# Modulation products on four quarters of TensorE's array, and products of ones at eleven places of a three-layer kernel

## The chip, the cores and the metric

One core of one Trainium2 chip runs the whole kernel in one launch. The metric is the device time of one execution in microseconds (us), as the median of several runs; lower is better.

## The reference

512 tokens of width 1024 (and 256 context tokens) go through a first block and then two layers of a second block, all in float32. Cut to what matters here:

```python
def first_block(x, c, ctx, c_ctx, w_mod, b_mod, ...):
    mod_x = (silu(c) @ w_mod + b_mod).reshape(-1, 6, d)       # 1024 x 6144
    mod_c = (silu(c_ctx) @ w_mod[:, :2*d] + b_mod[:2*d])
    hx = modulate(rms_norm(x, g_mix), mod_x[:, 0], mod_x[:, 1])   # h * (1 + scale) + shift
    hc = modulate(rms_norm(ctx, g_mix), mod_c[:, 0], mod_c[:, 1])
    x = x + mod_x[:, 2] * hybrid_mixer(hx, hc, ...)           # projections, three attentions, merge
    hx = modulate(rms_norm(x, g_ffn), mod_x[:, 3], mod_x[:, 4])
    x = x + mod_x[:, 5] * expert_choice_ffn(hx, ...)          # 16 experts take their top 64 tokens
    return rms_norm(x, g_final)

def second_block(x, c, ctx, c_ctx, mod_w, mod_b, ...):        # two layers
    for l in range(2):
        mod, mod_c = silu(c) @ mod_w[l] + mod_b[l], silu(c_ctx) @ mod_w[l] + mod_b[l]   # 1024 x 3072
        x, xc = trunk_layer(x, xc, mod, mod_c, ...)           # rmsnorm, modulate, projections, three
    return x                                                  # branches (mla, pool, gla), merge, residual
```

The modulation vectors (`mod`) are products of two vectors (c and c_ctx) with large weight matrices; everything that follows a norm needs its part of them.

## The kernel before, in words

**Layout.** The activations lie transposed: eight chunks of 128 features, each 128 x 512 tokens (`hx`, `x`), or 128 x 256 for the context (`hc`). A weight tile of 128 x 1024 float32 is loaded by the queue of SP, cut by ScalarE into a high part `wh` and by VectorE into the rest `wl`, and each product is three matmuls (`mm3`, L404 to L406): high by high, high by rest, rest by high. A projection is eight such triples into one PSUM tile. Matmuls on plain float32 (`modblock`, the norm sums, transposes, the router) are not split.

**Modulation.** `modblock` computes one block of `mod`: 16 weight tiles of 512 KB for a width of 2048 columns (8 tiles for 1024), 96 tiles in all. `sc` holds the two vectors padded to 32 columns, so that one matmul needs 32 of the array's 128 columns; a tile is multiplied in two matmuls of 512 columns (L471) whose results lie in PSUM rows 32j to 32j+31, with j alternately 0, 1 and 2, 3. Then ScalarE copies the sums to SBUF (`mrow`, L477), TensorE turns them (L480), VectorE adds the bias. The first block (16 tiles) runs at the start, ahead of everything that needs a modulated input; its tiles come through a ring of 7 buffers. Of the other 80 tiles, 56 are paced between the first block's projections (a ring of 3 buffers), and 24 between its merge and its output projection (a ring of 6).

**Order.** The code is a set of generators. `drain` runs one to its end; `weave`, `pace`, `alt` and `Fill` interleave two or more by estimated costs. A scheduler then orders the instructions of each engine by priority; each engine runs its own in that order and waits at an instruction whose inputs are not there. `s.late(...)` keeps an instruction where the program has it in relation to the others of its engine.

**Chains that TensorE waits for.** They are at the norms and at the router:
- `rstd_c` sums squares over features (L497), ScalarE and VectorE take the root and its reciprocal `rs`, TensorE transposes and spreads it (`bcast`, L533), ScalarE copies it to `rb`, and VectorE and ScalarE make `hx` of it (`normmod`, L567 to L570).
- `block1_mixer` (L1090 on) ends with `rstd_c`; `ffn_start` (L1261) then modulates, runs `router` (L1209, eight matmuls that lie on the four quarters in turn), turns the tokens back (L1278) and stores them to memory, and runs `topk` (eight rounds on VectorE, then four small matmuls L1252 and L1253). `experts` gathers the chosen tokens by a DMA with an index (`gather`, tile `xg`), turns them (`turn`, L1321) and runs the experts (L1306).
- `ffn_end` ends with `turned` and `rstd_col`; `xstart` (one for each layer of the second block, l = 0 and l = 1) spreads the root and makes `hx`. For l = 1 the sums (L516) come chunk by chunk behind the residual `o` (L2001, L2002), go through one row `sr` (L524), `rs` and L533.
- `xrest` ends with `merge(2, YG, ...)`, the merge of the gla branch: eight output chunks, each four triples of matmuls `ps<-yg,wh`. Three of the four `yg` inputs exist early; the fourth comes out of the last head of `gla` (L1910, L1911), its norm (L497, L533) and a split (L395).

Of the kernel before, what the change touches and what calls it, by code (L numbers as in the profile page):

```python
# [15 lines left out]
D = 1024  # L16
# [301 lines left out]
class Kern:  # L318
# [39 lines left out]
    def P1(s, tag, w=512):  # L358
        return s.pp.tile([128, w], F32, name=s.uid("ps"), tag=tag, bufs=PS[tag])

    def mm(s):
        return s.P1("mm")

# [96 lines left out]
    def modblock(s, sc, src, width, dst, bias, col0, big=None, ps=None):  # L460

        nc = s.nc
        ps = s.mm() if ps is None else ps
        nj = width // 512
        for k in range(8):
            for j in range(nj):
                if j % 2 == 0:
                    w = s.wp.tile([128, 1024], F32, name=s.uid("wr"), tag="wraw", bufs=NRAW) if big is None else \
                        big.tile([128, 1024], F32, name=s.uid("wm"), tag="wbig", bufs=s.nbig)
                    nc.sync.dma_start(w, src[k][:, j * 512:j * 512 + 1024])  # L470
                nc.tensor.matmul(ps[32 * j:32 * j + 32, :], sc[:, k, :], w[:, j % 2 * 512:j % 2 * 512 + 512],  # L471
                                 start=k == 0, stop=k == 7)
                if j % 2:
                    yield 0.9
        n = 32 * nj
        rows = s.T(nm="mrow", tag="t5")
        nc.scalar.copy(rows[:n], ps[:n])  # L477
        pt = s.at()
        for i in range(4):
            nc.tensor.transpose(pt[:, i * 128:i * 128 + n], rows[:n, i * 128:i * 128 + 128],  # L480
                                s.const("ident")[:n, :n])
        pv = pt.rearrange("p (i j v) -> p j i v", i=4, j=4)
        for v in range(2):
            o = dst[:, v, col0:col0 + 4 * nj].rearrange("p (j i) -> p j i", j=nj)
            b = bias[:, col0:col0 + 4 * nj].rearrange("p (j i) -> p j i", j=nj)
            nc.vector.tensor_tensor(o, pv[:, 0:nj, :, v], b, ALU.add)
        yield 0.5


# [600 lines left out]
    def block1_mixer(s, xd, M, ctx2):  # L1090
# [6 lines left out]
        rx = s.rstd_sb(s.sqsum(x, 512), D, 512)  # L1097
        with s.pool("bigA") as big:
            s.nbig = 7
            drain(s.modblock(sc, s.d["wmod0"], 2048, mod, bm, 0, big))  # L1100
        A1 = s.cp.tile([128, 2, 8], F32, name="A1")
        for v in range(2):
            nc.vector.scalar_tensor_tensor(A1[:, v, :], mod[:, v, 8:16], 1.0, s.const("gmix"), ALU.add, ALU.mult)
# [90 lines left out]
        def put(c, ps):  # L1194
            nc.vector.scalar_tensor_tensor(x[c], ps, m2h[:, c:c + 1], x[c], ALU.mult, ALU.add)
            s.load(xd[c], x[c])
            acc[0] = s.sqadd(acc[0], x[c], 512)
        drain(alt(s.outproj(hl, s.d["wout"], 512, put), mods, 2))
        return x, s.rstd_c(acc[0], D, 512)


# [32 lines left out]
    def topk(s):  # L1234
# [3 lines left out]
        for r in range(CAP // 8):  # L1238
            q = slice(8 * r, 8 * r + 8)
            nc.vector.max(vals[0:16, q], wk[0:16])  # L1240
            nc.vector.max_index(idx[0:16, q], vals[0:16, q], wk[0:16])
            nc.vector.match_replace(wk[0:16], vals[0:16, q], wk[0:16], -1.0)
            yield 2.0
        idf = A("idf")
        nc.vector.tensor_copy(idf[0:16], idx[0:16])
        s.gate, s.idx128 = A("gate", 8), s.cp.tile([128, 8], U32, name="idx128")
# [13 lines left out]
    def ffn_start(s, x, r):  # L1260

        nc = s.nc
        rb = s.T(nm="rb", tag="t5")
        nc.scalar.copy(rb, s.bcast(r, "t5"))
        yield 3.0
        for k in range(8):
            h = x[k]
            nc.vector.tensor_tensor(h, h, rb, ALU.mult)
            nc.scalar.activation(h, h, AF.Identity, bias=s.mod[:, 0, 24 + k:25 + k], scale=s.A2[:, k:k + 1])
            yield 0.6  # L1270
        h2 = x
        yield from s.router(h2)
        s.h2d = s.dram([512, D])
        for t in range(4):
            for g in range(2):
                pt = s.at()
                for j in range(4):
                    nc.tensor.transpose(pt[:, j * 128:j * 128 + 128], h2[4 * g + j][:, t * 128:t * 128 + 128],  # L1278
                                        s.const("ident"))
                o = s.T(nm="ht", tag="t5")  # L1280
                nc.scalar.copy(o, pt)
                nc.scalar.dma_start(s.h2d[t * 128:t * 128 + 128, g * 512:g * 512 + 512], o)
            yield 1.0
        yield from s.topk()

    def experts(s):
# [37 lines left out]
            return xe  # L1324

        xg = gather(0)
        xe = turn(xg)
        for p in range(8):
            if p < 7:
# [67 lines left out]
    def ffn_end(s, xd):  # L1397
# [25 lines left out]
            yield 1.2  # L1423

        s1, s2 = s.turned(ps, 2, 512, "ft")
        r1 = s.rstd_col(s1, D, 4)
        r2 = s.rstd_col(s2, D, 4, r1)
        rr = s.S("rr")
# [624 lines left out]
    def xstart(s, l, M, C, x, acc, xd, fill, done=None):  # L2053

        nc = s.nc
        if l == 0:
            rr, r1 = acc
            rb = s.T(nm="rb")
            nc.scalar.copy(rb, s.bcast(rr))
            a = s.cp.tile([128, 8], F32, name="Ag")  # L2060
            nc.vector.tensor_tensor(a, M["A"][:, 0, :], s.const("gfin"), ALU.mult)
        else:
            rb, a = s.T(nm="rb"), M["A"][:, 0, :]
            nc.scalar.copy(rb, s.bcast(s.rstd_col(s.turned(acc, 1, 512)[0], D, 4)))
        fill.step(5.0)
        hx = s.normmod(x, 512, a, M["S"][:, 0, 0:8], lambda: s.TT(512, "hx", "hx"), rb)
        fill.step(5.0)
# [14 lines left out]
    def xrest(s, l, M, C, hx, st, qn, gd, gt, xd, out, fill):  # L2082
# [14 lines left out]
        s.where2 = (None, {})  # L2097
        fill.flush()
        hl = []
        drain(s.merge(2, YG, s.d[f"wbr{l}"], gd, md, 512, hl, "hx"))  # L2100
        return s.finish(l, M, 0, hl, 512, lambda c: xd[c], (lambda c: xd[c]) if out is None else lambda c: out[:, c, :],
                        out is None)
# [113 lines left out]
```

## Time and profile before

| | before |
|---|---|
| time, median of 3 runs | 2761.48 us (2756.41 to 2765.88) |
| profiled execution: time | 2770.7 us |
| profiled execution: span on the core | 2768.9 us |
| mean granted TensorE clock over the span | 0.975 |
| TensorE busy | 95% of the span |
| VectorE, ScalarE, GpSimd busy | 57%, 44%, 6% |

The span is the stretch from the first to the last instruction of the core. The granted clock is a share of 2.4 GHz; 0.5 is 1.2 GHz. A matmul in float32 leaves two records in the trace, as do the transposes; a row that says x4 can be two matmuls.

### The profile page before, as it was taken

How to read it: one execution, taken by the hardware profiler on the slowest of the kernel's cores; microseconds unless marked ns; L12 is line 12 of the kernel's file. 1: busy time of each engine (PE TensorE's matmuls, PEld its weight loads, DVE VectorE, ACT ScalarE, POOL GpSimd, SP SyncE). 2: the span in 40 equal slices, each digit the busy share in tenths (PEclk: the TensorE clock that was granted, in tenths of full speed). 3: DMA queues.
4: the chain of work that ended last, by engine and by line, in shares of the span. 5: the costliest groups of instructions: out<-in, count | busy, mean ns of one | idle time of the engine just before them, and what ended most of it. 6: DMA issues, size and time to landing. Idle time of an engine off the chain costs nothing. (4 is left out here: it accounts for less than half of the span.)

```text
span 2768.9 us, 41759 instructions
## 1 busy us (share of the span) xinstructions
PE 2618.2 (95%) x16372; PEld 1858.0 (67%) x16372; DVE 1570.1 (57%) x2957; ACT 1230.5 (44%) x2159; POOL 159.6 (6%) x260
## 2 busy tenths in 40 slices
PE   6999999999968999998998899999999999999997
PEld 2666677887633566555654577777777777777776
DVE  3565576676451324455332665657976456766974
ACT  2333354445231224365222454546655544555652
POOL 1000001110001000000000000000010000000001
PEclk8899999999979999999999899999999999999998
DMA  8545424543979999988999332213453332114353
GB/s 281 180 162 202 141 81 173 187 134 121 326 289 336 351 392 353 335 312 292 354 374 380 119 117 74 77 54 136 136 192 129 123 122 82 57 47 137 119 175 116
DMA packets 167974, 537.68 MB, mean 194 GB/s; under 512 B 21272, under 2 KB 22376, under 8 KB 167776
## 3 DMA queue, kind: packets, MB, share of 16 engines
q1 hardware_dynamic: 138528, 460.40, 46.7%
q0 software_dynamic: 17152, 52.57, 5.9%
q10 hardware_dynamic: 12096, 22.03, 2.1%
q8 instruction: 129, 2.11, 0.3%
q14 instruction: 69, 0.57, 0.1%
HBM read 484.06 MB, written 48.76 MB: 192 GB/s over the span
## 5 line engine op out<-in xcount | busy, mean ns | idle before, releaser
L391 DVE TENSOR_TENSOR wl<-wr,wh 128x1024 fp32r<-128x1024 f32 x320 | 390.6, 1223 | 353.8 <-ACT wh L395 330.3
L395 ACT CAST wh<-wr 128x1024 fp32r<-128x1024 f32 x320 | 334.2, 1047 | 428.2 <-PE ps L405 339.8
L404 PE MATMUL ps<-hx,wh 128*128 128x512 f32 x1168 | 473.2, 406 | 5.8 <-ACT hx L569 5.1
L405 PE MATMUL ps<-hx,wh 128*128 128x512 f32 x1168 | 468.4, 401 | 0.1
L406 PE MATMUL ps<-hx,wl 128*128 128x512 f32 x1168 | 466.3, 400 | 0.0
L404 PEld LDWEIGHTS ps<-hx,wh 128*128 128x128 f32 x1168 | 221.7, 190 | 66.0 <-issue 12.4
L405 PEld LDWEIGHTS ps<-hx,wh 128*128 128x128 f32 x1168 | 221.4, 190 | 51.6 <-issue 8.0
L406 PEld LDWEIGHTS ps<-hx,wl 128*128 128x128 f32 x1168 | 221.3, 189 | 50.1 <-issue 5.0
L1306 PE MATMUL ps<-we,xe 128*64 128x512 f32 x1024 | 236.7, 606 | 10.5 <-DMA we<-in_wexp 10.5
L673 ACT ACTIVATE P<-ps,st 128x768 f32<-128x768 f32 (+3 forms) x144 | 111.1, 771 | 143.4 <-DVE st L669 107.3
L1306 PEld LDWEIGHTS ps<-we,xe 128*64 128x64 f32 x1024 | 72.8, 139 | 134.9 <-issue 112.9
L404 PE MATMUL ps<-hc,wh 128*128 128x256 f32 x496 | 144.7, 293 | 0.2 <-ACT wh L395 0.2
L406 PE MATMUL ps<-hc,wl 128*128 128x256 f32 x496 | 141.3, 285 | 0.7 <-DVE wl L391 0.6
L405 PE MATMUL ps<-hc,wh 128*128 128x256 f32 x496 | 141.4, 286 | 0.0
L667 DVE TENSOR_REDUCE st<-ps 128x1 f32<-128x768 f32 (+3 forms) x144 | 114.2, 793 | 36.0 <-PE ps L406 33.1
L1306 PE MATMUL ps<-we,hT 128*64 128x512 f32 x512 | 119.6, 612 | 6.6 <-DMA we<-in_wexp 5.2
L695 PE MATMUL ps<-c_ident,P 128*128 128x128 f32 x688 | 109.8, 278 | 5.3 <-ACT PT L698 3.5
L404 PEld LDWEIGHTS ps<-hc,wh 128*128 128x128 f32 x496 | 95.0, 192 | 20.3 <-issue 16.6
L695 PEld LDWEIGHTS ps<-c_ident,P 128*128 128x128 f32 x688 | 79.9, 140 | 39.6 <-ACT PT L698 13.4
L471 PE MATMUL ps<-wm,sc_cc 128*32 128x512 f32 x384 | 90.8, 664 | 16.1 <-DMA wm<-in_wmod 14.7
L698 ACT COPY PT<-ps 128x512 f32<-128x512 f32 x123 | 70.1, 586 | 72.8 <-PE ps L695 72.0
L405 PEld LDWEIGHTS ps<-hc,wh 128*128 128x128 f32 x496 | 95.2, 192 | 5.6 <-issue 5.2
(517 smaller groups left out, 5032.1 us busy)
## 6 DMA issues: line engine op xcount, KB each, us to landing
we<-in_wexp SPq DMA_DIRECT2D x384, 512.0 KB
wr<-in_win SPq DMA_DIRECT2D x240, 512.0 KB
wm<-in_wmod SPq DMA_DIRECT2D x48, 512.0 KB
wr<-in_wbr SPq DMA_DIRECT2D x48, 512.0 KB
dram<-th ACTq DMA_DIRECT2D x72, 256.0 KB
mth<-dram SPq DMA_DIRECT2D x72, 256.0 KB
wr<-in_wout SPq DMA_DIRECT2D x32, 512.0 KB
dram<-mth POOLq DMA_DIRECT2D x48, 256.0 KB, 3.4
```

The costliest lines, as they stand in the source:

```text
L391: s.nc.vector.tensor_tensor(out, a, b, ALU.subtract)
L395: i = s.nc.scalar.copy(hi, src)
L404: t.matmul(out, a[0], b[0], start=start, stop=False)
L405: t.matmul(out, a[0], b[1], start=False, stop=False)
L406: t.matmul(out, a[1], b[0], start=False, stop=stop)
L471: nc.tensor.matmul(ps[32 * j:32 * j + 32, :], sc[:, k, :], w[:, j % 2 * 512:j % 2 * 512 + 512], start=k == 0, stop=k == 7)
L667: nc.vector.tensor_reduce(st[:, 0:1], sc[:, :n], AX.X, ALU.max)
L673: nc.scalar.activation(p[:, :n], sc[:, :n], AF.Exp, bias=st[:, 1:2], scale=scale, accum_out=st[:, 2:3])
L695: nc.tensor.transpose(tp[:, j:j + 128], blocks[(i + j) // 128], s.const("ident"))
L698: nc.scalar.copy(parts[i // 512][:, :m], tp[:, :m])
L1306: nc.tensor.matmul(ps[64 * e:64 * e + 64, :], stat[:, k, 64 * e:64 * e + 64], ws[i][:, e * 512:e * 512 + 512], start=k == 0, stop=k == 7)
```

## The change

1. In `modblock` a weight tile is multiplied in four matmuls of 256 columns, one on each quarter of the array, in place of two of 512 columns on two quarters. The loop runs over the tile's place among the columns first and over the rows k inside it. The loads are of the same number and size. The copy `mrow` becomes 128 rows by 512 (or 256) columns, the turns are four (or two) of 128 x 128, and the bias adds of a 2048 block are four in place of two.
2. `warm(n)` issues n matmuls of 128 x 128 ones by ones into a PSUM tile of the tag "mm" (three buffers) that nobody reads, each kept in program order. There are 254 of them: 4 at each of the 17 stops of the first `modblock` and 8 behind it; 8 behind `block1_mixer`'s output projection; 10 in `ffn_start`; 50 in `topk`, ahead of the small matmuls; 50 in `experts` behind the first gather; 10 in `ffn_end`; 6 in `xstart` for l = 0, and 12 + 8 for l = 1; 12 in `xrest` of each layer, ahead of the last merge.

```diff
+    def warm(s, n):
+        ps = s.mm()
+        for _ in range(n):
+            s.late(s.nc.tensor.matmul(ps[:, 0:128], s.ones, s.ones, start=True, stop=True))
...
     def modblock(s, sc, src, width, dst, bias, col0, big=None, ps=None):
-        nj = width // 512
-        for k in range(8):
-            for j in range(nj):
-                if j % 2 == 0:
...
-                nc.tensor.matmul(ps[32 * j:32 * j + 32, :], sc[:, k, :], w[:, j % 2 * 512:j % 2 * 512 + 512],
-                                 start=k == 0, stop=k == 7)
+        nh = width // 1024
+        for h in range(nh):
+            for k in range(8):
+                w = big.tile([128, 1024], F32, name=s.uid("wm"), tag="wbig", bufs=s.nbig)
+                nc.sync.dma_start(w, src[k][:, h * 1024:h * 1024 + 1024])
+                for j in range(4):
+                    nc.tensor.matmul(ps[32 * j:32 * j + 32, h * 256:h * 256 + 256], sc[:, k, :],
+                                     w[:, j * 256:j * 256 + 256], start=k == 0, stop=k == 7)
+                yield 0.9
...
-            drain(s.modblock(sc, s.d["wmod0"], 2048, mod, bm, 0, big))
+            for _ in s.modblock(sc, s.d["wmod0"], 2048, mod, bm, 0, big):
+                s.warm(4)
+            s.warm(8)
...
+        s.warm(8)
         return x, s.rstd_c(acc[0], D, 512)
...
+        s.warm(50)
         idf = A("idf")
...
         nc.scalar.copy(rb, s.bcast(r, "t5"))
+        s.warm(10)
...
         xg = gather(0)
+        s.warm(50)
         xe = turn(xg)
...
         s1, s2 = s.turned(ps, 2, 512, "ft")
+        s.warm(10)
...
             nc.scalar.copy(rb, s.bcast(rr))
+            s.warm(6)
...
-            nc.scalar.copy(rb, s.bcast(s.rstd_col(s.turned(acc, 1, 512)[0], D, 4)))
+            sq = s.turned(acc, 1, 512)[0]
+            s.warm(12)
+            nc.scalar.copy(rb, s.bcast(s.rstd_col(sq, D, 4)))
+            s.warm(8)
...
         hl = []
+        s.warm(12)
         drain(s.merge(2, YG, s.d[f"wbr{l}"], gd, md, 512, hl, "hx"))
```

Line numbers of the changed kernel are 4 to 11 higher: L477 is the modulation matmul, L410 to L412 the triple, L501 the norm sum, L520 the sum of `o`, L528 and L537 the spreading, L365 the product of ones.

**TensorE behind the first modulation block.** Before, from the turn of `mrow` (L480) on; `wm` are tiles of the second block:

```order
L480 MATMUL ps_220<-c_ident,mrow_218 128x128 x4
L404 MATMUL ps_302<-hx_235,wh_298 128x512
L404 MATMUL ps_375<-hx_235,wh_371 128x512
L405 MATMUL ps_302<-hx_236,wh_298 128x512
L405 MATMUL ps_375<-hx_236,wh_371 128x512
L471 MATMUL ps_289<-wm_411,sc_cc 32x512 x2
L471 MATMUL ps_289<-wm_457,sc_cc 32x512 x2
L471 MATMUL ps_289<-wm_503,sc_cc 32x512 x2
L471 MATMUL ps_289<-wm_608,sc_cc 32x512 x2
L471 MATMUL ps_289<-wm_646,sc_cc 32x512
L406 MATMUL ps_302<-hx_235,wl_299 128x512
```

With the change, from the same turn (now L484) on:

```order
L484 MATMUL ps_332<-c_ident,mrow_330 128x128 x4
L365 MATMUL ps_341<-ones 128x128 x4
L365 MATMUL ps_346<-ones 128x128 x8
L477 MATMUL ps_417<-wm_539,sc_cc 32x256 x4
L410 MATMUL ps_430<-hx_363,wh_426 128x512
L410 MATMUL ps_503<-hx_363,wh_499 128x512
L477 MATMUL ps_417<-wm_587,sc_cc 32x256
L411 MATMUL ps_430<-hx_364,wh_426 128x512
L412 MATMUL ps_430<-hx_363,wl_427 128x512
L410 MATMUL ps_430<-hx_369,wh_426 128x512
```

Nine modulation matmuls (four and a half tiles) stood between the first triple's second and third matmul; now the third stands behind one tile and a quarter, and the tiles that follow are spread between the triples.

**TensorE at the end of layer l = 1.** Before, from the last 32 x 32 products of `gla` on:

```order
L1800 MATMUL ps_23877<-ql_21793,kl_23873 32x32 x16
L404 MATMUL ps_23942<-yg_22471,wh_23934 128x512
L405 MATMUL ps_23942<-yg_22471,wh_23934 128x512
L406 MATMUL ps_23942<-yg_22471,wl_23935 128x512
...
L497 MATMUL ps_23913<-ones,sq_23909 128x1 x4
L404 MATMUL ps_23994<-yg_22471,wh_23986 128x512
...
L533 MATMUL ps_23921<-c_ident,rs_23918 128x128 x4
```

With the change, from the last product of `gla`'s last head on:

```order
L1922 MATMUL ps_24367<-acc_24147,gv_22016 128x128
L501 MATMUL ps_24380<-ones,sq_24376 128x1 x4
L537 MATMUL ps_24388<-c_ident,rs_24385 128x128 x4
L365 MATMUL ps_24399<-ones 128x128 x12
L410 MATMUL ps_24422<-yg_22938,wh_24414 128x512
L411 MATMUL ps_24422<-yg_22938,wh_24414 128x512
```

Before, 27 matmuls of the last merge, all on the three early `yg`, stood between L1800 and L533. Now all of that merge stands behind L537 and the twelve products of ones. The end of layer l = 0 moves in the same way.

**TensorE at the start of layer l = 1.** Before, the last of the eight sums of `o` and what follows it (products of the context `hc` for its own layer):

```order
L516 MATMUL ps_18659<-sq_18759,ones 1x512
L404 MATMUL ps_18923<-hc_18360,wh_18919 128x256
L405 MATMUL ps_18923<-hc_18360,wh_18919 128x256
...
L524 MATMUL ps_18765<-c_ident,sr_18763 128x1 x4
L404 MATMUL ps_18923<-hc_18370,wh_18919 128x256
...
L404 MATMUL ps_18923<-hc_18380,wh_18919 128x256
L533 MATMUL ps_18773<-c_ident,rs_18770 128x128 x4
```

With the change, from the first context tile's last matmul on:

```order
L412 MATMUL ps_19143<-wh_19139,hc_18835 128x256
L520 MATMUL ps_19104<-sq_19172,ones 1x512
L520 MATMUL ps_19104<-sq_19180,ones 1x512
L520 MATMUL ps_19104<-sq_19188,ones 1x512
L520 MATMUL ps_19104<-sq_19196,ones 1x512
L520 MATMUL ps_19104<-sq_19204,ones 1x512
L528 MATMUL ps_19210<-c_ident,sr_19208 128x1 x4
L365 MATMUL ps_19215<-ones 128x128 x12
L537 MATMUL ps_19231<-c_ident,rs_19228 128x128 x4
L365 MATMUL ps_19237<-ones 128x128 x8
L410 MATMUL ps_19246<-wh_19133,hc_18800 128x256
```

The context products that lay between the sums, L524 and L533 stand behind the products of ones now; five sums follow one another with nothing between them.

## Rows read from the trace of the kernel before

**Rows 1.** The page: busy time of TensorE, and its busy tenths in 40 slices

```profile
PE 2618.2 (95%) x16372; PEld 1858.0 (67%) x16372; DVE 1570.1 (57%) x2957; ACT 1230.5 (44%) x2159; POOL 159.6 (6%) x260
...
PE   6999999999968999998998899999999999999997
```

**Rows 2.** Windows: stretch, busy us (instructions) by engine; granted clock, DMA share, GB/s

```profile
40.00:60.00 20.00, 14.80 (x39) 6.23 (x40) 12.55 (x18) 7.08 (x10) 0.00 (x0) 0.57 0.65 225
80.00:100.00 20.00, 13.44 (x51) 6.23 (x52) 13.71 (x30) 6.67 (x14) 0.00 (x0) 0.57 0.65 230
780.00:800.00 20.00, 15.74 (x66) 7.24 (x64) 8.11 (x16) 10.90 (x16) 0.54 (x1) 0.83 0.69 267
820.00:840.00 20.00, 8.25 (x38) 4.42 (x40) 4.11 (x15) 0.58 (x1) 2.02 (x2) 0.60 0.83 315
```

**Rows 3.** Waits of TensorE: line, what it waited for: us, times, longest

```profile
PE ps L471 <- DMA wm<-in_wmod: 14.7, 16, 2.6
```

**Rows 4.** Windows of the modulation matmuls L471 alone: stretch, TensorE, weight loads

```profile
100.00:330.00 230.00, 34.90 (x176) 5.47 (x176) 1.00 0.50 172
680.00:790.00 110.00, 21.16 (x96) 3.50 (x96) 1.00 0.78 269
```

**Rows 5.** Timeline of TensorE, start: start, us, line, [idle before <- releaser]

```profile
23.04 1.05 PE L471 MATMUL ps<-wm,sc_cc 128*32 128x512 f32 x4 [0.19 <-DMA wm<-in_wmod]
24.31 1.05 PE L471 MATMUL ps<-wm,sc_cc 128*32 128x512 f32 x4 [0.21 <-DMA wm<-in_wmod]
...
49.27 1.92 PE L471 MATMUL ps<-wm,sc_cc 128*32 128x512 f32 x4 [2.60 <-DMA wm<-in_wmod]
...
54.82 0.80 PE L406 MATMUL ps<-hx,wl 128*128 128x512 f32 x1
```

**Rows 6.** Timeline of TensorE from the router to the gathered tokens

```profile
792.71 6.40 PE L1209 MATMUL ps<-x,c_wrt 128*32 128x512 f32 x16 [2.25 <-ACT x L1269]
...
811.33 0.66 PE L1278 MATMUL ps<-c_ident,x 128*128 128x128 f32 x4 [1.12 <-ACT ht L1281]
821.21 0.36 PE L1252 MATMUL ps<-c_ident,vals 16*64 16x16 f32 x2 [9.23 <-DVE vals L1240]
822.78 0.39 PE L1253 MATMUL ps<-c_ident,idf 16*64 16x16 f32 x2 [1.21 <-DVE idf L1245]
...
833.10 1.94 PE L1321 MATMUL ps<-c_ident,xg 128*128 128x128 f32 x8 [8.93 <-DMA xg<-dram,idx]
```

**Rows 7.** Timeline of TensorE at the start of layer l = 0

```profile
1547.02 1.09 PE L533 MATMUL ps<-c_ident,rr 128*128 128x128 f32 x4 [1.86 <-DVE rr L1429]
...
1550.32 1.65 PE L404 MATMUL ps<-hx,wh 128*128 128x512 f32 x3 [1.36 <-ACT hx L569]
...
1556.38 0.39 PE L404 MATMUL ps<-hx,wh 128*128 128x512 f32 x1
```

**Rows 8.** Timeline of TensorE at the end of layer l = 1

```profile
2678.32 0.50 PE L404 MATMUL ps<-yg,wh 128*128 128x512 f32 x1
...
2682.97 0.39 PE L1910 MATMUL ps<-qx,st 128*128 128x128 f32 x2
2683.19 0.39 PE L1911 MATMUL ps<-acc,gv 128*128 128x128 f32 x2
...
2687.76 0.39 PE L406 MATMUL ps<-yg,wl 128*128 128x512 f32 x1
2688.00 0.60 PE L533 MATMUL ps<-c_ident,rs 128*128 128x128 f32 x4
2690.81 0.96 PE L404 MATMUL ps<-yg,wh 128*128 128x512 f32 x3 [2.22 <-ACT yg L395]
```

**Rows 9.** Timeline of VectorE, then of TensorE, at the start of layer l = 1

```profile
2153.16 1.22 DVE L391 TENSOR_TENSOR wl<-wr,wh 128x1024 fp32r<-128x1024 f32 x1 [7.20 <-ACT wh L395]
...
2164.91 0.60 PE L533 MATMUL ps<-c_ident,rs 128*128 128x128 f32 x4
...
2168.14 0.51 PE L404 MATMUL ps<-hx,wh 128*128 128x512 f32 x1 [1.69 <-ACT hx L569]
```

More of the change, by code (lines that the diff above doesn't have):

```diff
@@ L463, in modblock @@
         ps = s.mm() if ps is None else ps
-        nj = width // 512
-        for k in range(8):
-            for j in range(nj):
-                if j % 2 == 0:
-                    w = s.wp.tile([128, 1024], F32, name=s.uid("wr"), tag="wraw", bufs=NRAW) if big is None else \
-                        big.tile([128, 1024], F32, name=s.uid("wm"), tag="wbig", bufs=s.nbig)
-                    nc.sync.dma_start(w, src[k][:, j * 512:j * 512 + 1024])
-                nc.tensor.matmul(ps[32 * j:32 * j + 32, :], sc[:, k, :], w[:, j % 2 * 512:j % 2 * 512 + 512],
-                                 start=k == 0, stop=k == 7)
-                if j % 2:
-                    yield 0.9
@@ L475, in modblock @@
-        n = 32 * nj
+        nh = width // 1024
[7 more added lines that the diff above has]
+                yield 0.9
@@ L476, in modblock @@
         rows = s.T(nm="mrow", tag="t5")
-        nc.scalar.copy(rows[:n], ps[:n])
+        nc.scalar.copy(rows[:, :256 * nh], ps[:, :256 * nh])
         pt = s.at()
[L479 to L486, printed above, removed]
+        for i in range(2 * nh):
+            nc.tensor.transpose(pt[:, i * 128:i * 128 + 128], rows[:, i * 128:i * 128 + 128], s.const("ident"))
@@ L487, in modblock @@
+        for h in range(nh):
+            pv = pt[:, h * 256:h * 256 + 256].rearrange("p (i j v) -> p j i v", i=2, j=4)
+            c = slice(col0 + 8 * h, col0 + 8 * h + 8)
+            for v in range(2):
+                nc.vector.tensor_tensor(dst[:, v, c].rearrange("p (j i) -> p j i", j=4), pv[:, :, :, v],
+                                        bias[:, c].rearrange("p (j i) -> p j i", j=4), ALU.add)
         yield 0.5
```

## The prediction

> **What bounds the kernel now.** I read the page first, for the engine that is busy: TensorE is, 95% of the span, and its busy tenths are 9 nearly everywhere; the gaps are in the first 70 us, around 800, 1500 and at the end [rows 1]. So in most of the span a matmul taken away is time taken away, and a matmul added is time added, unless it stands in a gap. Then I read the windows, for the gaps and the clock. In 40–60 and in 80–100 TensorE is busy for 14.80 and 13.44 of 20 us and its granted clock is 0.57: most of both stretches is at 1.2 GHz; 780–800 and 820–840 have 0.83 and 0.60 [rows 2]. The waits say what it waits for in the first 100 us: modulation tiles, 14.7 us in 16 waits [rows 3]. The timelines give the price of a matmul at either clock and, around each place of the change, the chain that ends last [rows 5 to 9].
>
> **The prices.** The two 128 x 128 float32 products L1910 and L1911 start 0.22 us apart at full clock [rows 8]; a product of ones has that shape, so I take 0.22 us, and twice that at 1.2 GHz. A lone product of 512 columns would be four times that, 0.88. A modulation tile is two of these, and 44 tiles take 34.90 us in 100–330 (0.79 each) and 24 take 21.16 in 680–790 (0.88 each) [rows 4]: the two products on two quarters run side by side, entirely. Four of 256 columns would then take 0.44 if all four quarters run side by side, 0.88 if only two do.
>
> **The modulation in the full stretches.** There TensorE has nothing to wait for (tenths 9 [rows 1]), so each of the 68 tiles gives back what it gets shorter: 0.4 x 68 = 27 us if the four overlap, 0 if they go two by two. Evidence between the two: the router's eight 512-column products lie on four quarters in turn. They take 6.40 us, although they wait for ScalarE between them, in 780–800, whose mean clock of 0.83 is that of 6.8 us at 1.2 GHz and the rest at 2.4, and I put the low part at this run, the one of the stretch with waits in it [rows 2, 6]. One by one they would take 8 x 1.76 = 14.1, in pairs 7.0. So at least 2.2 run at once: more than two quarters do overlap. I take −27, nearest to the pairs, which overlap entirely; the weak ends are 2.2 at once (0.80 a tile, −6) and 0.
>
> The Trainium skill speaks less well of it: "TensorE: Matmul & The Clock Gate", section "Measured speedup vs the span model", has three column tiles at 2.38 times one, not 3. By that factor a tile would take 4 x 0.44 / 2.38 = 0.74 us, an estimate from that page, and the 68 tiles would give back some 6 to 10 us. The pairs here, which lose nothing, don't agree with a loss of a fifth.
>
> **The first 100 us.** In the first block a tile comes each 1.27 us and takes 1.05 [rows 5]. With the change it is about 0.5 plus four products of ones, 0.9: 1.4, so this stretch is level to +2 us. Behind it the order changes: before, four and a half tiles stand ahead of the first L406, and TensorE waits for two that have not landed (2.60 us for one at 49.27), at 1.92 us for a tile, the price of the low clock, so that the L406 starts only at 54.82 [rows 5]. Now that matmul stands behind one and a quarter tiles, and the projection can go on as `hx` comes. The stretch 41–55 holds 5 to 9 us of this; VectorE, 12.55 of 20 us busy in 40–60, then sets the pace [rows 2]. Of the 14.7 us of waits [rows 3] the first block's are 0.2 each [rows 5], some 2 in all, so 12 us lie in the two stretches of low clock. In 80–100 they are for tiles that the loads have to bring anyway, and only the shorter products (up to 1 us a tile at 1.2 GHz) come off. Together I take −8; bounds 0 (the loads set the end in both) and −14.
>
> **The router, the top 64 and the gather.** The first fifty products take 11 us at full clock. The last turn before them ends at 812.0, and the index numbers are needed at 822.78 (L1253) [rows 6]: they end at 823.0 at full clock and 3 or 4 us later if the clock is low when they begin, so 0 to +4. The second fifty start when the small matmuls are through, about 824.2, and end at 835.3; the gathered tokens are there at 833.10: +2.2. Against that stand the turns of the tokens (1.94 us at low clock, half at full [rows 6]) and the first expert matmuls. The ten in `ffn_start` lie in the wait of 2.25 us ahead of the router [rows 6]; with the eight ahead of the norm I put them at −0.5. I take +2; from −2 to +8.
>
> **The start of layer l = 0.** From 1547.02 to 1556.38 the clock is low: the spreading takes 1.09 for four records, where at full clock it is 0.60 [rows 8], and fourteen matmuls from 1550.32 to 1556.38 take 0.43 each, as against 0.23 [rows 7]. The ten and the six products fill the waits of 1.86 and 1.36 us and the one between. If the clock then stays up, 14 x 0.2 + 0.5 = 3.3 us come back; 16 products overrun a wait by a few tenths. I take −3; from −4.5 to +2.
>
> **The two ends, l = 0 and l = 1.** Here the change takes cover away. Before, 27 matmuls of the last merge, from 2678.32 to 2687.76, run while the chain of the last head goes on [rows 8]; they were not late, they were the filler. Now they are queued behind L537 and twelve products of ones. 27 x 0.23 = 6.2 us come behind the chain. The chain itself has less in front of its norm sum and its spreading, up to 1.5 us, and the twelve products (2.6 us) fit in the wait of 2.22 us plus the spreading. That is +4.7 at full clock. But with its filler gone TensorE does next to nothing for some 9 us, and the rows at the start of l = 0 show what follows such a stretch: 1.2 GHz. Then the twelve products take 5.3 us and the first merge matmuls 0.43. So +5 to +12 each; I take +6 each, +12 in all.
>
> **The start of l = 1.** Before, context products fill the chain of `o`; the price was that VectorE's `wl` waited 7.20 us for a buffer that TensorE freed late, with two chunks of `o` behind it, and L533 came at 2164.91 [rows 9]. Now one context tile (24 matmuls) stands before L528 and the rest behind the last product of ones. The chain can end some 8 to 12 us earlier, but the work that is left is the same, and TensorE has waits of 5 to 8 us in the chain and 20 products (4.4 us); the 1.69 us wait for `hx` [rows 9] goes. I take +6; from 0 to +12.
>
> **The sum.** −27 − 8 + 2 − 3 + 12 + 6 = −18 us. Against the profiled execution (2770.7 us, span 2768.9) that is 2753; that execution is 9 us above the median of the runs, 2761.48, and I apply the difference to the median: 2743.
>
> **The rivals.**
>
> Rival A, the quarters go two by two, or 2.2 at once: the modulation tile stays at 0.8 to 0.88. For it: nothing in the trace has four quarters at more than 2.2 at once; and the weight loads, 5.47 us in 44 tiles [rows 4], double in number. Against it: pairs lose nothing. Then the sum is −18 + 21 to 27 = +3 to +9: 2764 to 2770, no change or a little slower. The factor of the Trainium skill's page "TensorE: Matmul & The Clock Gate" gives a case between this one and the forecast, −1 to +3.
>
> Rival B, the barriers cost more than the clock gives (slower). Each product of ones holds back all later matmuls; where a chain runs without filler the clock falls, and the following 5 to 10 us of work takes twice the time. That makes each of the ends and the start of l = 1 cost +12 to +14 in place of +6, and both fifties, at low clock, +4 and +8. With the rest at its value the sum is −38 + 3 x 13 + 12 = +13: 2774. It decides for slower by over 8 us from 15 us at each of the three places, or from 12 where the fifties run long. For it: 95% busy means that there is little waiting to fill. Against it: at these places the twelve products run exactly before the dense work.
>
> Rival C, everything bites: the quarters give 27, the first 100 us give 14, and the clock stays up at the ends (+4.7 each, start of l = 1 at 0): −27 − 14 − 2 − 4.5 + 9.4 = −38: 2723.
>
> Rival D, the clock does not react: products of ones leave the low stretches as they are, because the waits around them still let it fall. It costs the −3, and some of the first 100 us: sum about −10, 2751, still faster by 0.4%.
>
> **How the numbers follow.** A run of this kernel can tell about 0.3%, 8 us, from no change. The forecast (four quarters overlap, the three barriers at +4 to +9) has 0.50 and 2735 to 2752; C 0.15; D 0.10; A 0.15; B 0.10. Faster by over 0.3%: nearly all of the forecast and of C, most of D: 0.73. Slower: B and a third of A: 0.13. Within: 0.14. The range takes in C, D and the near part of A: 2715 to 2767.
>
> **What would show each step.** In the profile after, the modulation matmuls by windows: 44 tiles in some 20 us, as against 34.90, is the main term; 30 or more is rival A. The clock of 40–60 and of 80–100 rising to 0.8 or more, and the waits for `wm` falling below 14.7 us, show the first 100 us. The products of ones in `topk` should end within 1 us of the index numbers, and those behind the gather 2 us after the tokens. At both ends a gap of several us before L501 and L537 shows the lost filler. The prediction would be wrong above all if the quarters don't overlap, or if the low clock stretches grow at the three barriers.

## The result, and the profile after

The changed kernel takes 2786.34 us (median of 7 runs, 2773.98 to 2791.71), the kernel before 2765.9 us in the same comparison (7 runs, 2756.41 to 2768.94). The ratio is 1.007, with a 95% interval of 1.005 to 1.0089: 20 us slower, where 18 us faster was forecast. The profiled execution has a span of 2782.4 us, 13.5 us more than before.

The page after, busy times, and TensorE's clock in 40 slices of the span:

```profile
PE 2649.6 (95%) x17260; PEld 1924.2 (69%) x17260; DVE 1571.5 (56%) x2967; ACT 1231.0 (44%) x2159; POOL 159.9 (6%) x260
...
PEclk9899999999999999999999999999999999999999
```

TensorE is busy 31 us longer than in [rows 1], although the modulation got shorter. The windows of the changed kernel (stretch, busy time of TensorE, weight loads, VectorE, ScalarE, GpSimd, then granted clock, DMA share, GB/s):

```profile
40.00:60.00 20.00, 18.10 (x124) 11.03 (x117) 14.54 (x25) 8.87 (x12) 1.61 (x3) 1.00 0.64 219
80.00:100.00 20.00, 14.33 (x87) 10.08 (x88) 15.21 (x33) 7.27 (x16) 0.00 (x0) 0.58 0.52 187
820.00:840.00 20.00, 19.65 (x94) 8.06 (x94) 1.83 (x3) 1.18 (x2) 0.00 (x0) 1.00 0.88 327
2040.00:2060.00 20.00, 15.45 (x79) 13.97 (x79) 6.04 (x12) 5.78 (x12) 0.00 (x0) 0.83 0.43 139
2680.00:2700.00 20.00, 14.86 (x173) 12.86 (x173) 8.17 (x14) 8.00 (x14) 0.00 (x0) 0.91 0.44 149
```

The clock is whole in 40–60 and in 820–840, where it was 0.57 and 0.60 [rows 2]; it is still 0.58 in 80–100, and it now falls at the two ends of the layers, 2040–2060 and 2680–2700.

**The modulation.** The modulation matmuls alone, by the same windows as [rows 4]:

```profile
100.00:330.00 230.00, 26.24 (x358) 9.12 (x358) 1.00 0.51 177
680.00:790.00 110.00, 14.08 (x192) 4.80 (x192) 0.98 0.84 308
```

8.7 and 7.1 us less, 15.7 where 27 was forecast. How this came about is seen in three groups of the kernel before (timeline of TensorE, start, duration, line, and the matmul that follows each):

```profile
135.63 1.05 PE L471 MATMUL ps<-wm,sc_cc 128*32 128x512 f32 x4
136.61 0.50 PE L404 MATMUL ps<-qk,qk 128*128 128x512 f32 x1
...
144.49 1.07 PE L471 MATMUL ps<-wm,sc_cc 128*32 128x512 f32 x8
145.49 0.50 PE L404 MATMUL ps<-hx,wh 128*128 128x512 f32 x1
...
776.75 1.91 PE L471 MATMUL ps<-wm,sc_cc 128*32 128x512 f32 x8
778.59 0.50 PE L404 MATMUL ps<-mh,wh 128*128 128x512 f32 x1
```

One tile (x4) holds TensorE for 0.98 us, from its start to that of the next matmul. Two tiles in a row (x8) hold it for 1.00 at 144.49: in a block of 2048 columns the old loop took the two column halves of one k in turn, j = 0, 1 and then 2, 3, so two tiles in a row already lay on all four quarters and ran side by side. At 776.75 two tiles hold it for 1.84: the last eight tiles of each of the two stretches belong to a block of 1024 columns, which has j = 0, 1 only, and so two quarters. After the change a tile takes 0.57 and two take 1.01:

```profile
132.07 0.64 PE L477 MATMUL ps<-wm,sc_cc 128*32 128x256 f32 x8
132.64 0.50 PE L410 MATMUL ps<-qk,qk 128*128 128x512 f32 x1
...
140.52 1.07 PE L477 MATMUL ps<-wm,sc_cc 128*32 128x256 f32 x16
141.53 0.50 PE L410 MATMUL ps<-hx,wh 128*128 128x512 f32 x1
```

So a pair in a block of 2048 columns gained nothing; the trace has twelve of these that stand by themselves, 24 of the 68 tiles. A tile that stands alone gained 0.41 us, and so did a third tile behind such a pair. The 16 tiles of the two blocks of 1024 columns gained wherever they stood, 7.1 of the 15.7 us (L471 in 295–330 and 760–790 is busy 8.03 and 8.48 us before, L477 in 288–330 and 745–790 4.70 and 4.69 after).

**The start.** The first modulation block and what follows it, timeline of TensorE after:

```profile
23.06 0.64 PE L477 MATMUL ps<-wm,sc_cc 128*32 128x256 f32 x8
23.62 1.16 PE L365 MATMUL ps<-ones 128*128 128x128 f32 x8
24.71 0.64 PE L477 MATMUL ps<-wm,sc_cc 128*32 128x256 f32 x8
...
43.29 2.84 PE L365 MATMUL ps<-ones 128*128 128x128 f32 x24
...
46.69 0.73 PE L410 MATMUL ps<-hx,wh 128*128 128x512 f32 x2
```

A tile with its four products of ones takes 1.65 us (23.06 to 24.71). The loads bring one each 1.27 us [rows 5], so the block waits for TensorE now, and the first triple for twelve more products of ones.

**Router, top 64 and gather**, to be held against [rows 6]:

```profile
775.23 5.98 PE L1216 MATMUL ps<-x,c_wrt 128*32 128x512 f32 x16
...
794.45 12.35 PE L365 MATMUL ps<-ones 128*128 128x128 f32 x100
806.73 0.28 PE L1260 MATMUL ps<-c_ident,vals 16*64 16x16 f32 x2
...
807.85 11.43 PE L365 MATMUL ps<-ones 128*128 128x128 f32 x100
819.12 1.04 PE L1330 MATMUL ps<-c_ident,xg 128*128 128x128 f32 x8
```

The router starts 17.5 us earlier than in [rows 6], the turn of the gathered tokens 14.0 us earlier. Neither block of fifty is followed by a wait: each ends after what it was to bridge.

**The start of layer l = 0** (with [rows 7]), and the next wait:

```profile
1530.66 0.60 PE L537 MATMUL ps<-c_ident,rr 128*128 128x128 f32 x4
...
1563.61 0.47 PE L410 MATMUL ps<-ukv,kvn 128*128 128x512 f32 x1 [2.45 <-DVE kr L1509]
```

**The end of layer l = 1**, with [rows 8]:

```profile
2687.84 0.49 PE L1921 MATMUL ps<-qx,st 128*128 128x128 f32 x2 [1.69 <-DVE ad L1855]
2689.49 0.49 PE L1922 MATMUL ps<-acc,gv 128*128 128x128 f32 x2 [1.16 <-ACT acc L1859]
...
2692.65 1.05 PE L501 MATMUL ps<-ones,sq 128*128 128x1 f32 x8 [1.33 <-ACT sq L1925]
2694.53 1.09 PE L537 MATMUL ps<-c_ident,rs 128*128 128x128 f32 x4 [0.83 <-DVE rs L512]
2695.41 3.99 PE L365 MATMUL ps<-ones 128*128 128x128 f32 x24
2699.16 0.48 PE L410 MATMUL ps<-yg,wh 128*128 128x512 f32 x1
```

Four waits, 5.0 us, where [rows 8] show merge matmuls without a gap; then twelve products of ones in 3.75 us, which begin at the low clock (L537 takes 1.09), and only then the first of the merge's matmuls. **The start of layer l = 1**, with [rows 9]:

```profile
2152.11 1.02 PE L520 MATMUL ps<-sq,ones 128*1 128x512 f32 x2 [2.42 <-ACT sq L519]
...
2154.13 2.94 PE L365 MATMUL ps<-ones 128*128 128x128 f32 x24
2156.91 0.60 PE L537 MATMUL ps<-c_ident,rs 128*128 128x128 f32 x4
```

and VectorE there:

```profile
2146.71 0.69 DVE L2013 TENSOR_TENSOR o<-o,xr 128x512 f32<-128x512 f32 x1 [3.39 <-DMA xr<-dram]
2150.70 0.69 DVE L2013 TENSOR_TENSOR o<-o,xr 128x512 f32<-128x512 f32 x1 [3.31 <-DMA xr<-dram]
2154.53 0.18 DVE L512 RECIPROCAL rs<-rs 128x4 f32<-128x4 f32 x1 [3.14 <-ACT rs L511]
```

The chain of `o` no longer waits for a split weight, as it did [rows 9]; it waits for the residual `xr` to be loaded, twice for over 3 us, and the spreading stands 2.2 us behind `rs` because the twelve products run first. From the first chunk of `o` on VectorE to the spreading it is 23.8 us (2133.11 to 2156.91), before 29.2 (2135.76 to 2164.91).

**Where the time went.** For each matmul of TensorE I took its start minus that of the same matmul before (same line, same tiles, same place in the sequence), and of these the median over 20 us. Negative is earlier. Here are the changed kernel and the kernels of the next section at some points of the kernel before:

```
start of the 20 us   100    340    780    920   1480   1560   1600   1980   2100   2220   2620   2740
the change          -2.7  -11.3  -17.6  -12.8  -15.5  -19.1  -15.2  -12.0   -2.6    5.3    7.0   14.1
quarters_only      -11.4  -17.6  -24.6  -25.5  -29.0  -28.0  -28.2  -28.1  -26.5  -27.8  -27.7  -25.9
ones_only            9.0    8.8    7.4   13.9   10.6    5.6    9.5    9.4   20.5   27.1   30.1   40.7
without_three       -2.5  -10.6  -17.2  -13.1  -18.0  -24.8  -19.3  -19.6  -17.2  -18.9  -18.9  -15.7
one_each            -1.7   -9.7  -16.1  -13.7  -12.0  -13.6   -8.1   -8.4   -0.9    6.1    7.8   14.9
without_start      -10.6  -17.6  -24.1  -22.6  -20.5  -24.6  -20.6  -17.3   -8.6   -0.5   -0.3   11.9
without_fifties     -3.4  -11.9  -18.4  -18.1  -18.7  -23.4  -18.9  -16.4   -4.7    2.5    3.1   15.5
quarters_three     -10.1  -16.7  -23.5  -24.2  -24.2  -23.3  -22.7  -19.5  -10.5   -1.1    3.4   12.7
quarters_three_free -10.5 -17.2  -23.7  -21.1  -23.0  -26.1  -20.4  -20.1  -18.1   -8.9   -7.4   -4.8
quarters_l0        -10.3  -16.7  -23.0  -23.5  -24.5  -29.7  -25.4  -25.3  -23.9  -23.7  -22.9  -20.5
halves_by_column    -2.7    2.1    4.7    6.5    5.2    1.0    0.8    0.9    2.2    1.3    1.4    3.1
```

One profile each: where two kernels have the same order the columns still differ by up to 6 us (the change and without_three at 1560). So a step of 3 us in one row is no finding. Nor is a profiled execution the median one: those of quarters_three, one_each and quarters_three_free took 11, 6 and 5 us more than the median of their runs, those of quarters_only and halves_by_column 5 and 7 less. The verdicts below go by the timed runs where these can tell. The row of the change reads: 2.7 won at the start, 14.9 in the modulation up to the router, 4.8 lost at the router and in the first expert weights; then 9.4 lost between 1980 and 2100, 8.0 from there to 2220, 7.1 at the second end.

### The profile page after: what moved, and what is told of

The parts are those of the page before. It is cut to its first block, busy times and chain, and to the rows that moved or that the text cites. A ratio compares the mean times of both kernels' runs of the same rounds, so it can differ in the third digit from the quotient of the medians.

```text
span 2782.4 us, 43541 instructions
## 1 busy us (share of the span) xinstructions
PE 2649.6 (95%) x17260; PEld 1924.2 (69%) x17260; DVE 1571.5 (56%) x2967; ACT 1231.0 (44%) x2159; POOL 159.9 (6%) x260
## 5 line engine op out<-in xcount | busy, mean ns | idle before, releaser
L410 PE MATMUL ps<-hx,wh 128*128 128x512 f32 x1168 | 472.8, 405 | 1.8 <-ACT wh L401 1.1
L412 PE MATMUL ps<-hx,wl 128*128 128x512 f32 x1168 | 466.5, 400 | 0.0
L410 PEld LDWEIGHTS ps<-hx,wh 128*128 128x128 f32 x1168 | 220.9, 189 | 58.3 <-issue 9.9
L412 PEld LDWEIGHTS ps<-hx,wl 128*128 128x128 f32 x1168 | 221.2, 189 | 48.7 <-issue 3.1
L412 PE MATMUL ps<-hc,wl 128*128 128x256 f32 x496 | 141.4, 286 | 3.0 <-DVE wl L397 2.9
L410 PE MATMUL ps<-hc,wh 128*128 128x256 f32 x496 | 143.7, 290 | 0.2 <-ACT wh L401 0.2
L410 PEld LDWEIGHTS ps<-hc,wh 128*128 128x128 f32 x496 | 94.6, 191 | 18.9 <-issue 14.9
L412 PEld LDWEIGHTS ps<-hc,wl 128*128 128x128 f32 x496 | 94.5, 191 | 5.1 <-DVE wl L397 4.0
```

Of the source, the lines that this page charges most:

```text
L410: t.matmul(out, a[0], b[0], start=start, stop=False)
L412: t.matmul(out, a[1], b[0], start=False, stop=stop)
```

## The experiments

### The two parts apart

`quarters_only` takes every product of ones out of the changed kernel, `ones_only` takes the modulation back to the form of before:

```diff
-            for _ in s.modblock(sc, s.d["wmod0"], 2048, mod, bm, 0, big):
-                s.warm(4)
-            s.warm(8)
+            drain(s.modblock(sc, s.d["wmod0"], 2048, mod, bm, 0, big))
...
-        s.warm(8)
-        s.warm(50)
...
```

> The four-quarter modulation alone, with none of the products of ones. Theory: two tiles that follow one another already lie on all four quarters in the kernel before, so only tiles that stand alone get shorter, by 0.41 us; some 14 us less up to the router, ratio about 0.995. Rival (all 68 tiles of the full stretches shorter by 0.4 us): 27 us less, ratio 0.990. Rival (the quarters cost at the ends, the products of ones are not to blame): as slow as the full change, ratio 1.005 or more.

Measured: 2749.68 us against 2769.32 before, ratio 0.994 (0.9924 to 0.9957). The quarters alone make the kernel 17 us faster by the ratio, 20 by the medians. The table shows 11.4 us of it in the first 100 us, 13.2 us between there and the router (the theory has 14) and next to nothing after. The rival with 27 us in the full stretches is out by the table, the one with a loss by the time; the whole gain is above the theory's, since the start gives more than it said.

> The products of ones alone, with the modulation of before. Theory (barriers and added products cost): 20 to 30 us slower than before, ratio 1.007 to 1.011, since the gain of the quarters is gone. Rival (the products are harmless and the quarters are what costs): ratio 1.000.

Measured: 2802.88 us, ratio 1.0123 (1.0106 to 1.014), 34 us slower, a little above the theory's range. The products of ones are what costs: −17 and +34 by the ratios make +17, against +19 (14 to 25 by the interval) of the two together.

### The three places where filler stands behind them

`without_three` takes out the 12 ahead of each last merge and the 12 and 8 at the start of layer l = 1; `one_each` leaves one in place of each of these numbers.

```diff
-        s.warm(12)
         drain(s.merge(2, YG, s.d[f"wbr{l}"], gd, md, 512, hl, "hx"))
...
-            s.warm(12)
             nc.scalar.copy(rb, s.bcast(s.rstd_col(sq, D, 4)))
-            s.warm(8)
```

> The full change without the products of ones at the three places where they hold back filler: the 12 ahead of each last merge and the 12 and 8 at the start of layer 1. Theory: 22 us less than the full change (7.9 and 6.3 at the two merges, 8 at the start of layer 1), ratio to before about 0.999. Rival (the loss is spread over the low clock stretches elsewhere): no better than the full change by more than 5 us.

Measured: 2758.06 us, ratio 0.9962 (0.9948 to 0.9977): 30 us less than the full change by the ratios (28 by the medians of two comparisons), faster than the kernel before, and more than the theory's 22. The loss is at these places.

> The full change with a single product of ones at each of those places in place of 12, 12, 12 and 8. The order of TensorE is that of the full change. Theory (the place in the order costs, since the filler stands behind it): it keeps at least half of the 22 us, ratio 1.003 to 1.007. Rival (the time of the 40 products themselves costs): it is as fast as the kernel without them, ratio about 0.999.

Measured: 2778.9 us, ratio 1.0032 (1.0019 to 1.0045). So 40 of the 44 products gone bring some 10 us by the ratios, and 19 of the 30 stay with a single product at each place. In the table `one_each` loses 7.5, 7.0 and 7.1 us at the three, which is what the full change loses less 3. Its end of layer l = 1:

```profile
2694.38 1.87 PE L501 MATMUL ps<-ones,sq 128*128 128x1 f32 x8 [1.34 <-ACT sq L1925]
2696.91 1.08 PE L537 MATMUL ps<-c_ident,rs 128*128 128x128 f32 x4 [0.66 <-DVE rs L512]
2697.79 0.63 PE L365 MATMUL ps<-ones 128*128 128x128 f32 x2
2698.07 0.77 PE L410 MATMUL ps<-yg,wh 128*128 128x512 f32 x1
```

The waits are those of the full change, and no merge matmul comes ahead of L365. By the runs the place in the order costs two thirds and the products one third; by the table the place costs more, 21.6 of 24.5.

### The same products, pinned or not, with the quarters alone

`quarters_three` is `quarters_only` with the products of ones at the three places; `quarters_three_free` leaves out the call that keeps them in program order:

```diff
-            s.late(s.nc.tensor.matmul(ps[:, 0:128], s.ones, s.ones, start=True, stop=True))
+            s.nc.tensor.matmul(ps[:, 0:128], s.ones, s.ones, start=True, stop=True)
```

> The four quarters and, of the products of ones, only those at the three places: 12 ahead of each last merge, 12 and 8 at the start of layer 1, each kept in program order as in the full change. Theory (at these three places the change loses what it loses most): 22 to 28 us slower than the quarters alone, ratio to before 1.002 to 1.004. Rival (the three places cost so much only together with the other products of ones): under 12 us slower than the quarters alone, ratio below 0.999.

Measured: 2771.35 us against 2771.36, ratio 1.0005 (0.9991 to 1.002): 18 us more than the quarters alone by the ratios (0.994), below the theory's 22 and above the rival's 12. These three places alone take back all that the quarters give.

> The same 44 products of ones at the same three places, but not kept in program order: the scheduler puts them between the matmuls of the chain, and 24 of the 27 merge matmuls run ahead of or beside the norm as before. Theory (the loss is the filler that the pinned products hold back): at most 10 us slower than the quarters alone, ratio 0.994 to 0.998. Rival (the time of the products and of the tile that they need is what costs): as slow as with the pinned ones, ratio 1.002 or more.

Measured: 2760.29 us, ratio 0.9949 (0.9932 to 0.9966), 15 us less than pinned by the ratios, 11 by the medians: inside the theory's range, and the rival is out. At the two ends the products are in the chain's own waits, and the merge runs beside the norm as before:

```profile
2672.39 1.83 PE L365 MATMUL ps<-ones 128*128 128x128 f32 x14
...
2674.49 1.28 PE L365 MATMUL ps<-ones 128*128 128x128 f32 x10
```

The table has the ends at +2.0 and +2.6 (pinned: +9.0 and +9.3). The start of layer l = 1 still costs 9 us there, pinned or not: the 20 products stand among the last sums of `o`, and the context matmuls behind them as in the pinned kernel.

### How tiles ran side by side before

`halves_by_column` is the kernel before with the two loops exchanged. A tile stays two products of 512 columns on two quarters, but the tiles that follow one another use the same two.

```diff
-        for k in range(8):
-            for j in range(nj):
...
+        for h in range(nj // 2):
+            for k in range(8):
...
+                for j in range(2 * h, 2 * h + 2):
+                    nc.tensor.matmul(ps[32 * j:32 * j + 32, :], sc[:, k, :], w[:, j % 2 * 512:j % 2 * 512 + 512],
```

> The kernel before with the two loops of the modulation exchanged and nothing else: a tile is still two products of 512 columns on two quarters, but eight tiles that follow one another use the same two quarters, where before they alternated. Theory (before, two tiles in a row ran side by side on all four quarters): they now run one behind the other, 0.85 us more for each of some 20 such pairs in the full stretches, 15 to 22 us slower, ratio 1.006 to 1.008. Rival (only products of one tile overlap, and a tile of before cost 0.8 us wherever it stood): no difference, ratio 1.000.

Measured: 2779.96 us, ratio 1.0041 (1.0028 to 1.0054), 11 us slower: the sign is the theory's, the size is below it. The timeline has the mechanism:

```profile
160.11 1.91 PE L470 MATMUL ps<-wm,sc_cc 128*32 128x512 f32 x8
161.95 0.50 PE L404 MATMUL ps<-hx,wh 128*128 128x512 f32 x1
...
170.05 1.07 PE L470 MATMUL ps<-wm,sc_cc 128*32 128x512 f32 x8
171.05 0.38 PE L404 MATMUL ps<-hc,wh 128*128 128x256 f32 x1
```

Two tiles on the same quarters hold TensorE for 1.84 us; at 170.05, where the eighth tile of a block is followed by the ninth, the first of the other column half, they still take 1.00. The modulation matmuls in 100–330 are busy 42.01 us, as against 34.90 [rows 4]. Twelve pairs stood by themselves on four quarters, not the twenty that I counted, and 0.84 us for each is 10. In the table only 3 us are left at 2740, from a profiled execution that is 7 us under the median of its runs.

### The start, the fifties, layer l = 0

`without_start` takes the 76 products of ones out of the first modulation block, `without_fifties` the two blocks of fifty; the rest is the full change. `quarters_l0` is `quarters_only` with the 10 and 6 at the start of layer l = 0. In `quarters_fitted` products of ones stand only in waits that nothing else fills, in the numbers that its expectation lists.

> The full change without the 76 products of ones in the first modulation block. Theory (they make the first block wait for TensorE, 1.66 us a tile where the loads bring one in 1.27, and 12 more stand ahead of the first triple): 8 us less than the full change, ratio to before 1.004. Rival (they keep the clock up at 40 to 58 us and are worth it): no less than the full change, ratio 1.007 or more.

Measured: 2781.75 us, ratio 1.0034 (1.0015 to 1.0052), some 10 us less than the full change by the ratios. In the table it is 7.9 us ahead of the full change at 100, and 2.2 at 2740. The rival is out: the clock of 40–60, whole in the full change, falls back to 0.65 without these products, and the kernel is faster. First the window of this kernel, then two of `quarters_only`:

```profile
40.00:60.00 20.00, 17.04 (x77) 9.52 (x76) 14.51 (x22) 7.71 (x10) 0.00 (x0) 0.65 0.72 245
...
40.00:60.00 20.00, 16.20 (x79) 10.09 (x80) 14.19 (x20) 6.69 (x9) 0.00 (x0) 0.74 0.65 226
80.00:100.00 20.00, 18.61 (x133) 15.94 (x132) 11.45 (x25) 9.08 (x18) 0.00 (x0) 0.80 0.57 188
```

In 80–100 the quarters alone have a clock of 0.80 without any product of ones, and the full change 0.58.

> The full change without the two blocks of fifty products of ones. Theory (the first ends 1.4 us late, the second 2.2 us late, and the expert weights come later with them): 4 to 6 us less than the full change, ratio to before 1.005. Rival (they return what they cost by the clock of the turns and the first expert products): no difference, ratio 1.007.

Measured: 2784.81 us, ratio 1.0054 (1.0035 to 1.0074). That is the theory's number, but the interval holds the rival's too: not decided by the time. In the table the full change loses 4.8 us from 780 to 920, this kernel 0.4, but at 2740 nothing of that is left (14.1 and 15.5).

> The four quarters, and products of ones only where TensorE waits and nothing else could run: none at the start, at the two merges and at layer 1; 36 and 28 in place of the two fifties (7.9 and 6.2 us at 0.22 each, in waits of 9.1 and 7.5), 7 in place of 10 in the end of the experts, the 8, 10 and 6 as they are. Theory (they fit in the waits and keep the clock up behind them): 2 to 6 us less than the quarters alone, ratio to before 0.992. Rival (the clock falls at the next wait and what is won is lost there): the same as the quarters alone, ratio 0.994.

```diff
-        s.warm(50)
+        s.warm(36)
         idf = A("idf")
...
-        s.warm(50)
+        s.warm(28)
         xe = turn(xg)
```

Measured: 2750.56 us, ratio 0.9927 (0.9909 to 0.9945), against 0.994 for the quarters alone (2749.68). No difference that these runs tell.

> The four quarters and, of the products of ones, only the 10 and 6 at the start of layer 0. Theory (they keep the clock up for the first hx products, 3.5 us by the ledger of the full change, and the wait for kr that follows takes it back): the same as the quarters alone within 2 us, ratio 0.993 to 0.995. Rival (the clock kept is time won, as the prediction has it): 3 us less than the quarters alone, ratio 0.993 or less.

Measured: 2752.64 us, ratio 0.9933 (0.9918 to 0.9948): the quarters alone again, though the interval doesn't exclude the rival's 3 us. Its timeline shows what becomes of the gain:

```profile
1520.03 0.60 PE L537 MATMUL ps<-c_ident,rr 128*128 128x128 f32 x4
...
1553.33 0.67 PE L410 MATMUL ps<-ukv,kvn 128*128 128x512 f32 x1 [2.79 <-DVE kr L1503]
```

The spreading runs at the full clock and the table has 5.2 us won from 1480 to 1560; 2.9 of them lie ahead of the first product of ones (the turn of `sr`, 1517.36 here, 1544.76 before), 2.3 behind it. At 1553 TensorE waits 2.79 us for `kr`, a wait that `quarters_only` does not have there, at a clock of 0.83 in 1550–1560 (1.00 there), and 4.3 us are gone by 1600. The full change shows the same (−15.5, −19.1, −15.2). Why `kr` comes no earlier is in the traces too. VectorE has it behind the split of `uk`, for which it waits 4.45 us (`quarters_only` 1.29), since ScalarE waits 4.01 for the load of `uk` (0.84). GpSimd issues that load; before, and in `quarters_l0`:

```profile
1566.34 0.54 POOL L384 DMA_DIRECT2D uk<-in_ukv  x1 [0.74 <-DMA dram<-xo]
...
1538.86 0.54 POOL L390 DMA_DIRECT2D uk<-in_ukv  x1 [0.74 <-DMA dram<-xo]
```

It is 21.6 and 21.5 us behind the turn of `sr`, waiting for the stores of `xo`, whatever the clock of TensorE; `kr` starts 34.8 and 35.1 us behind that turn.

## Why the prediction was wrong, step by step

**The modulation in the full stretches (−27): the size was wrong, and the step is "each of the 68 tiles gives back what it gets shorter".** The four quarters do run side by side, as forecast: a tile takes 0.57 us where one that stood alone took 0.98. But I read 0.79 and 0.88 us a tile out of busy times of whole stretches [rows 4] as the price of every tile. They are means of several kinds: tiles that stand alone, at 0.98, pairs in blocks of 2048 columns that shared the array, at 0.50 a tile, and pairs in blocks of 1024 columns, at 0.92. The second kind could not gain. The timeline would have shown it; `halves_by_column` shows that the sharing was there. The term is −13 (`quarters_only`, from 100 to 780 us), some 0.23 us of busy time a tile (15.7 by 68) and not 0.4; the 44 tiles of 100–330 took 26.24 us, between the 20 of the forecast and the 30 of rival A. Rival A, that only two quarters run at a time, is out, and so is the factor of 2.38 for three column tiles in the Trainium skill's page "TensorE: Matmul & The Clock Gate", section "Measured speedup vs the span model", as a bound here: two tiles, eight products that I estimate at 0.44 us if one by one, take 1.01, 3.5 at once.

**The first 100 us (−8).** Two errors of opposite sign. The quarters, with the order that comes with them, are worth more here than I took, 11 us in `quarters_only`. The products of ones in the first block cost 8 of these, where I had "level to +2": four of them with a tile take 1.65 us, not 1.4, since both shapes take 0.1 to 0.2 us more beside each other than in a long row (four products of ones 1.09, four times 0.22 are 0.88; a tile 0.57, half of a pair 0.50). That moved the block past the pace of the loads. Of the signs that I named for this stretch two came: the clock of 40–60 rose to 1.00, and the waits for `wm` fell from 14.7 us to 5.3. They were worth less than the delay: `without_start` waits 16.0 us for `wm` and is faster. The third did not come, 80–100 stayed at 0.58. One reading was wrong too: the first block's waits [rows 3, 5] add up to 3.6 us, since one of them is 1.46, and not to 2.

**The router (+2).** The index numbers come some 1.4 us late (from the end of the last turn to the turn of `idf`, L1253, 10.8 us before [rows 6], 12.2 after), the tokens' turn 1.9 (10.3 from L1253 before, 12.3 after), as the working had it for the second; the table has 4.8 lost by 920. The direction was right, the size inside the bounds; the time does not settle it.

**The start of layer l = 0 (−3).** The gain came (2.3 of the 3.6 us that the table has from 1480 to 1560, the rest lies ahead of the products) and was gone 30 us later. The step that failed is the silent one, that a stall removed stays removed: `kr`, the next thing that TensorE waits for, came no earlier, and TensorE reached it earlier. `kr` stands behind the load of `uk`, which is issued at the same distance from the start of this chain in both kernels. The working priced the clock there and named no other engine.

**The two ends and the start of layer l = 1 (+18).** The mechanism was right, filler that is held back, and the size was too low: 24.5 us by the table, 30 by the ratio of `without_three`. Of that 19 us stay when only one product stands at each place. The ends have the waits and the low clock of rival B. At the start of layer l = 1 the chain got 5.4 us shorter, where I had 8 to 12; it has a wait that I had not seen, for the residual's loads.

**The sum.** −13 in place of −27 and 0 in place of −3 make 17; the start (−3 in place of −8), the three places (24 to 30 in place of 18) and the router (5 in place of 2) make another 14 to 20. From −18 that leads to +13 to +19, between the span's +13.5 and the +20 of the medians. Rival B came nearest, by place if not by price: its 13 us at each place were 7 to 9.5 in the table, and it had the gain of the quarters whole. That its 2774 lies nearer to the measured time than the other cases is in part luck: its gain and its loss were both too large. One chance was added up wrong: slower, by B and a third of A, is 0.15 and not 0.13.

## What to carry to other kernels

A product that nobody reads, pinned in the program's order, is a fence: price first what the scheduler had put into the wait, then the product. A busy engine's mean over a stretch hides which instructions already share it; look at two neighbours on the timeline before multiplying a saving by a count. No kernel here is told apart as faster than the quarters without any product of ones (0.994; `quarters_fitted` 0.9927, `quarters_l0` 0.9933, with intervals that overlap).

## What was unexpected of the hardware

In the old form two modulation tiles on four quarters hold TensorE for 1.00 us where one holds it for 0.98: the second costs next to nothing. A whole clock can cost more than it gives: with the products of ones the clock of 40–60 is 1.00 and without them 0.65, and the kernel is some 10 us faster without. And two kernels that have the same order up to 1980 differ by 6 us at 1560, with waits of 6.6 and 4.4 us for expert weights and clocks of 0.91 and 1.00 in 1480–1500, so that a single trace can't price an edit of 3 us.
